# Layer 1's head outputs scaled and turned by VectorE, placed by DMA, with the gates written into the tiles of the gated outputs

## The chip, the cores and the metric

One core of a Trainium2 chip runs the whole program in one launch. The metric is the device time of that launch in microseconds (us). Before the change it was 1343.44 us, the median of 3 runs (1340.47 to 1344.24).

## The reference, cut to what matters

The program is one step of a trunk with two layers, on 512 prompt tokens and 32 sample tokens, 1024 wide, in float32. Layer 0 is an RWKV-7 layer and layer 1 is a differential attention layer with 12 heads of 128. Only layer 1 is touched:

```python
def diff_layer(x, mk, mv, k_past, v_past, layer_idx, norm_w, w_out, w_in, ...):
    h = rmsnorm(x, norm_w)
    q, k, v, qm, gate = jnp.split(h @ w_in, [...], axis=-1)
    ...
    attn = probs(q1, k1) - lam * probs(q2, k2)
    o = einsum('bhqk,bkhd->bqhd', attn, v_all)
    o = rmsnorm(o, subln) * (1.0 - lam_init)
    y_mem = mem_attention(qm, mk, mv)
    out = jnp.concatenate([o, y_mem], axis=-1) * jax.nn.silu(gate)
    return x + out @ w_out, k, v
```

What the change concerns is the last part: each head's output `o` (512 tokens by 128 values) is divided by its root mean square, turned from token-major to value-major, multiplied by `subln` and by the gate, and then used in the product with `w_out`. The four memory heads (`y_mem`) share the same engines and queues.

## The kernel before, in words

**Projections.** A projection of 128 columns is one `block` (L1947): its weights come in two loads of 256 KB each (`load`, L271; tile `raw`, five buffers), ScalarE rounds each half to a short form (`whi`), VectorE subtracts to get the rest (`wlo`; `split`, L300, two buffers of each, one buffer is a whole block's weights), and TensorE runs 48 matmuls `ps_g` of 272 columns: two halves of the tokens, eight slices of the depth, and three products for each (high by high, high by low, low by high). A `raw` buffer may be loaded again once the `wlo` made from it has been written.

**Pieces between matmuls.** The other work of layer 1 is cut into steps (Python generators), and `block` runs a step ahead of the matmul whose number is listed for it, so `step(end, 8)` means: the next step of `end` ahead of the block's matmul 8. TensorE and SyncE are "tied" in this layer (`tie`, L123): they keep the order in which the program was written. For VectorE and ScalarE the tile framework's scheduler picks the order. On the chip each engine then works through its list in order, and SyncE, which issues nearly all DMAs, does so too.

**Groups.** `groups` (L1958) runs three groups of four heads. In each, the key, query and value blocks of the four heads come first, and the attention of a head (scores `ps_s`, softmax, transposes `ps_aT`, product `ps_o`) is spread over the blocks that follow. Then come the blocks of gates. In groups 0 and 1: gate of head 0, query of a first memory head, gates of heads 1 and 2, query of a second memory head, gate of head 3, and the gates of the two memory heads. In group 2 there are no memory heads: gates of heads 0 to 3, after which the product with `w_out` begins, and the ties of TensorE and SyncE are lifted after the gate of head 0.

**The sample tokens.** `diff_end` (L2253) handles the 32 sample tokens of the four heads together: softmax of their scores `ssb`, transposes `ps_saT`, the product `ps_os`, its root mean square (a short chain of one-column steps on VectorE: `os`, `nt`), the scaling `os<-os,os`, a transpose `ps_osT` on TensorE, and a copy `osT`.

**The heads' outputs.** The last part of `diff_end`, here called fin, is asked once per head. VectorE scales the four 128x128 squares of the head's output `ot` by the reciprocal root mean squares (columns of `oss`), TensorE transposes the four squares into PSUM (`ps_oT`), and VectorE multiplies the result by `subs` (named `dv` in the profile's rows) and by the gate `sg` into the gated output `og` (the tile `o1[g]`, 128 values by 544 tokens); a small product does it for the sample tokens. The gate itself (`gate_evac`, L1072) is written by ScalarE (tanh) and VectorE into one of two buffers `sg`.

**Memory heads.** `mem_steps` (L1252) makes the scores of a memory head in three tiles (`ps_mm`: two tiles of 256 tokens, and one of the samples with `cmk`), their softmax (`mnm`, `mp`, `mrs`), and for the first two tiles a transposition in squares of 32 by VectorE (`mpq`). `placed` (L131) writes such a tile to DRAM with four DMAs that put every square of 32 where it belongs (scratch `mprob`), and one DMA fetches the whole turned tile (`mpT`). The product `ps_mo` takes `mpT` with the memory values `mhv` and `cmv`, whose loads SyncE issues beside them. `small_out` and `moved` in `diff_head` (L2056) turn attention probabilities in the same way.

Of the kernel before, what the change touches and what calls it, by code (L numbers as in the profile page):

```python
# [9 lines left out]
F32 = mybir.dt.float32  # L10
# [4 lines left out]
ALU = mybir.AluOpType  # L15
AX = mybir.AxisListType

P = 128
D = 1024
KT = D // P  # L20
TP = 512
# [4 lines left out]
MIXW = 1536  # L26
# [12 lines left out]
SGB = 2  # L39
# [69 lines left out]
class Trunk:  # L109
# [962 lines left out]
    def gate_evac(self, n):  # L1072
        nc = self.nc
        sg = self.sg[n % SGB]

        def evac(ps, v):
            self.ae.activation(sg[:, v], ps, AF.Tanh, scale=0.5)
            gated = lambda: self.ve.scalar_tensor_tensor(sg[:, v], sg[:, v], 1.0, ps, ALU.add, ALU.mult)
            if not self.ordered:
                return gated()  # L1080
            done.append(self.put_off(gated, 0.43))
            return gated

        done = []

        def get():
            self.until(done[-1])
            return sg

        return sg, get, evac  # L1090

    def gate(self, src, c0):

        self.gates += 1
        sg, _, evac = self.gate_evac(self.gates)
        self.proj(src, c0, evac)
        return sg

    def dest(self, g, sg):

# [390 lines left out]
    def layer0(self, mem):  # L1491
        nc, o = self.nc, self.o
        w = self.a["rw_in"][0]
# [4 lines left out]
        with ExitStack() as ctx:  # L1498
# [43 lines left out]

            def add_gate(pr, st, c0, n):
                def make(wt):
                    sg, st["gate"], evac = self.gate_evac(n)
                    yield from self.steps(wt, evac)
                add(pr, w, c0, make)

# [19 lines left out]
            mems, came, made = [{} for _ in range(MH)], [], {}  # L1568
# [104 lines left out]
            for pr in range(NPAIR):  # L1673
# [9 lines left out]
                t, left, spent = 0.0, each[pr] - kept, 0.0  # L1683
# [156 lines left out]
    def layer1(self):  # L1840
# [7 lines left out]
        with ExitStack() as ctx:  # L1848
            with ExitStack() as c2:
                self.dfp = p = self.pool("df", 1, ctx=c2)  # L1850
                m1 = c2.enter_context(ExitStack())
                mp = self.pool("mem1a", 1, ctx=m1, side="right")

                nlam = self.nlam
                self.vscr = [self.dp.tile([TP, P], F32, name=f"vscr{i}") for i in range(2)]
                self.ascr = [self.dp.tile([TP, P], F32, name=f"ascr{i}") for i in range(4)]
                self.bscr = [self.dp.tile([3 * P, P], F32, name=f"bscr{i}") for i in range(2)]
                self.mprob = [self.dp.tile([TP, P], F32, name=f"mprob{i}") for i in range(4)]
                self.qs = [p.tile([P, P], F32, name=f"qs{i}") for i in range(2)]
                for t in self.qs:  # L1860
                    nc.gpsimd.memset(t[:], 0.0)  # L1861
                self.kz = [p.tile([P, 2, T], F32R, name=f"kz{i}") for i in range(2)]
                for t in self.kz:
                    for m in range(2):
                        r = slice(64 - 64 * m, P - 64 * m)
                        nc.gpsimd.memset(t[r, m, :].bitcast(F32), 0.0)
                pe, early = [], iter(order[:MADE])

                def aside():
                    if pe:  # L1870
                        made.update({g: self.gated(g, *self.fetch(pe[0], g)) for g in islice(early, 2)})

                def free():
                    m1.close()
                    pe.append(self.pool("wo1e", 1, ctx=ctx, side="right"))

                self.groups(w, p, mp, nlam, aside, free)
# [65 lines left out]
            for _ in self.w_out(1, p, order, consume, o=made)[0]:  # L1943
                pass
        self.hctx.close()

    def block(self, w, c0, evac, pieces=()):  # L1947
# [10 lines left out]
    def groups(self, w, p, mp, nlam, aside, free):  # L1958

        late = []  # L1960
        for hg in range(3):
            gr = self.diff_group(hg, p)
            heads = [self.diff_head(gr, j, p, nlam) for j in range(4)]
            sgs, fins, prev = [], [], None
            step = lambda it, *at: [(i, lambda: next(it, None)) for i in at]

            turns = lambda it, last: step(last, 2) + step(it, 6) + step(last, 10) + step(it, 20, 26) + step(last, 30) + step(it, 36, 47)

            def gate(c0, pieces):
                self.gates += 1  # L1970
                sg, _, evac = self.gate_evac(self.gates)
                self.block(w, 3 * MIXW + 512 + c0, evac, pieces)
                return sg

            for j, (parts, it) in enumerate(heads):
                h = 4 * hg + j
                before = step(prev, 4, 14, 36, 42) if j else late
                if j > 1:
                    before = before[:2] + step(heads[j - 2][1], 22, 30) + before[2:]
                k, q, v = parts()  # L1980
                self.block(w, MIXW + h * P, k, before)
                if not j and hg == 2:
                    free()
# [12 lines left out]
                prev = it  # L1996
            end = self.diff_end(gr, nlam)
            fin = lambda j, at: (at, lambda: end.send((j, sgs[j])))
            g0 = 4 * hg * P
            sgs.append(gate(g0, step(prev, 4, 14) + step(heads[2][1], 22, 30) + step(prev, 36, 42)))  # L2000
# [20 lines left out]
            sgs.append(gate(g0 + P, step(prev, 4) + step(end, 8) + step(prev, 14) + step(end, 28)))  # L2021
            sgs.append(gate(g0 + 2 * P, step(m0, 14, 14) + step(end, 16) + [fin(0, 22)] + step(m0, 28, 28) + step(m1, 30, 30) + [fin(1, 38)]))
            self.block(w, 3 * MIXW + st1["c"], query(st1), step(m0, 4, 14, 14) + step(m1, 20) + step(m0, 28, 40))
            sgs.append(gate(g0 + 3 * P, [fin(2, 10)] + step(m1, 22, 22, 36, 36)))
            sg0 = gate(MIXW + st0["c"], [fin(3, 10)])
            st0["gate"] = lambda sg0=sg0: sg0
            sg1 = gate(MIXW + st1["c"], step(m0, 8) + step(m1, 16, 26, 26, 38))
            st1["gate"] = lambda sg1=sg1: sg1
            late = step(m1, 8, 22)

# [222 lines left out]
    def diff_end(self, gr, nlam):  # L2253
# [39 lines left out]
        ask = yield  # L2293
        while True:
            j, sg = ask
            on = gr["on"][j]
# [8 lines left out]
            ask = yield  # L2305

    def combine(self, pt, rs, n, nlam):

# [78 lines left out]
```

## Time and profile before

| | |
|---|---|
| median of 3 runs | 1343.44 us |
| the profiled execution's own time | 1343.22 us |
| its span | 1341.3 us |
| mean granted TensorE clock | 0.997 |
| instructions in the trace | 31455 |
| DMA packets, bytes | 472324, 170.78 MB |

The profile is of one execution. Its times count in us from the start of the span. Each row of a timeline has the start, the length, the engine (PE is TensorE, DVE is VectorE, ACT is ScalarE, SPq is SyncE's issuing of DMAs), the line, the operation with what it writes and reads, and how many instructions of the kind follow one another (x). Where the engine stood still ahead of a row, the idle time and what ended it stand in brackets. Nearly all rows have line 106, since a helper records the operations, so the tile names tell them apart. Matmuls are pipelined: a row's length overlaps the next row, and what a matmul costs is the distance between starts.

### The profile page before, as it was taken

The numbers are of one execution on the slowest core, as the hardware profiler recorded it, in microseconds if no ns is written. First come the engines' busy times: TensorE is split into PE (matmuls) and PEld (weight loads), VectorE is DVE, ScalarE is ACT, GpSimd is POOL, SyncE is SP. The second block draws the span as 40 slices with busy tenths as digits, with TensorE's granted clock in tenths as the row PEclk, the third lists the DMA queues.
The fourth block names the chain that finished last, engine by engine and source line by source line (L and its number), as shares of the span: only waits on it lengthen the run. The fifth ranks groups of instructions, "written<-read, shape, count | busy, mean of one in ns | idle before, by whom it ended". The sixth has DMA issues, their size and how long they took to land. (4 is left out here: it accounts for less than half of the span.)

```text
span 1341.3 us, 31455 instructions
## 1 busy us (share of the span) xinstructions
PE 1305.8 (97%) x11507; PEld 1248.3 (93%) x11507; DVE 975.8 (73%) x2393; ACT 797.3 (59%) x2244; POOL 364.0 (27%) x833
## 2 busy tenths in 40 slices
PE   8999999999999999999999999999999999999997
PEld 6988899999999998888999999999999999999997
DVE  5776788888888888675754478877588758887343
ACT  5765678877787777565543376654466536664222
POOL 2127668666776668600000000000000001002000
PEclk9999999999999999999999999999999999999999
DMA  7454344445443444443375466764487464872321
GB/s 226 146 146 108 90 105 99 103 104 119 95 118 91 115 113 99 113 141 90 99 197 135 128 199 154 164 154 119 113 185 178 100 159 111 184 158 89 95 84 71
DMA packets 472324, 170.78 MB, mean 127 GB/s; under 512 B 244857, under 2 KB 462722, under 8 KB 472170
## 3 DMA queue, kind: packets, MB, share of 16 engines
q1 hardware_dynamic: 472106, 168.76, 50.2%
q8 instruction: 91, 1.49, 0.5%
q14 instruction: 63, 0.52, 0.1%
q10 hardware_dynamic: 64, 0.02, 0.0%
HBM read 128.16 MB, written 40.34 MB: 126 GB/s over the span
## 5 line engine op out<-in xcount | busy, mean ns | idle before, releaser
L106 PE MATMUL ps_g<-hh,wlo 128*128 128x272 f32 x1808 | 537.0, 298 | 1.0 <-DVE wlo L106 0.9
L106 PE MATMUL ps_g<-hl,whi 128*128 128x272 f32 x1808 | 534.8, 297 | 1.0 <-DVE hl L106 0.7
L106 PE MATMUL ps_g<-hh,whi 128*128 128x272 f32 x1808 | 528.9, 293 | 1.2 <-DVE ats L106 0.8
L106 PEld LDWEIGHTS ps_g<-hh,whi 128*128 128x128 f32 x1808 | 341.0, 189 | 4.9 <-DVE ats L106 1.0
L106 PEld LDWEIGHTS ps_g<-hl,whi 128*128 128x128 f32 x1808 | 340.7, 189 | 5.0 <-DVE hl L106 1.9
L106 PEld LDWEIGHTS ps_g<-hh,wlo 128*128 128x128 f32 x1808 | 340.5, 189 | 3.1 <-DVE wlo L106 1.7
L106 DVE TENSOR_TENSOR wlo<-raw,whi 128x512 fp32r<-128x512 f32 x314 | 215.5, 698 | 102.2 <-ACT whi L106 99.9
L106 ACT CAST whi<-raw 128x512 fp32r<-128x512 f32 x314 | 189.0, 619 | 117.0 <-PE ps_g L106 56.0
L881 POOL TENSOR_TENSOR tm<-u,m 102x84 f32<-102x84 f32 (+23 forms) x341 | 143.4, 421 | 118.8 <-DMA m<-sc 67.8
L883 POOL TENSOR_TENSOR u<-u,tm 102x84 f32<-102x84 f32 (+23 forms) x341 | 152.8, 448 | 26.7
L106 PE MATMUL ps_g<-hi,wlo 128*128 128x272 f32 x512 | 147.7, 288 | 1.4 <-DVE wlo L106 1.4
L106 PE MATMUL ps_g<-hi,whi 128*128 128x272 f32 x512 | 147.8, 289 | 0.0
L106 PE MATMUL ps_g<-lo,whi 128*128 128x272 f32 x512 | 147.5, 288 | 0.0
L1390 POOL TENSOR_TENSOR lo<-og,hi 128x544 fp32r<-128x544 f32 x8 | 13.2, 1653 | 374.2 <-ACT hi L106 373.8
L106 PEld LDWEIGHTS ps_g<-hi,wlo 128*128 128x128 f32 x512 | 96.4, 188 | 1.8 <-DVE wlo L106 1.8
L106 PEld LDWEIGHTS ps_g<-hi,whi 128*128 128x128 f32 x512 | 96.5, 189 | 0.2 <-ACT whi L106 0.2
L106 PEld LDWEIGHTS ps_g<-lo,whi 128*128 128x128 f32 x512 | 96.4, 188 | 0.2 <-DVE lo L106 0.2
L106 ACT ACTIVATE pt<-ps_s,snm 128x128 f32<-128x128 f32 (+3 forms) x96 | 50.3, 527 | 63.7 <-DVE snm L106 63.7
L106 DVE SCALAR_TENSOR_TENSOR SB<-ps_c,dl,sd 64x64 f32<-64x64 f32 x168 | 47.4, 282 | 23.3 <-PE ps_c L106 21.0
L106 ACT COPY sv<-ps_c 64x64 f32<-64x64 f32 x192 | 39.6, 206 | 33.7 <-PE ps_c L106 31.8
L106 ACT ACTIVATE sg<-ps_g 128x272 f32<-128x272 f32 x64 | 25.1, 394 | 45.7 <-PE ps_g L106 41.4
L1861 POOL MEMSET qs<- 128x128 f32 x2 | 0.3, 205 | 190.6 <-PE ps_g L106 190.6
(399 smaller groups left out, 2480.5 us busy)
## 6 DMA issues: line engine op xcount, KB each, us to landing
raw<-in_rw_in_dram SPq DMA_DIRECT2D x114, 256.0 KB
raw<-in_df_in_dram SPq DMA_DIRECT2D x112, 256.0 KB
raw<-in_w_out_dram SPq DMA_DIRECT2D x64, 256.0 KB
tscr<-bt SPq DMA_DIRECT2D x48, 128.0 KB
bt<-tscr SPq DMA_DIRECT2D x12, 512.0 KB
oscr<-sg SPq DMA_DIRECT2D x16, 272.0 KB
lo<-oscr SPq DMA_DIRECT2D x16, 272.0 KB
m<-sc SPq DMA_DIRECT2D x33, 128.0 KB
```

The source lines that it names most:

```text
L106: return lambda *a, **k: self.trunk.tie(self, issue(*a, **k))
L881: nc.gpsimd.tensor_tensor(tm[:, :n, :wd], u3[:, :n, kx : kx + 1].to_broadcast(sh), m3[:, kx : kx + 1, kx + 1 :].to_broadcast(sh), ALU.mult)
L883: nc.gpsimd.tensor_tensor(u3[:, :n, kx + 1 :], u3[:, :n, kx + 1 :], tm[:, :n, :wd], ALU.add)
L1390: (self.nc.gpsimd if g % 2 and self.o1 else self.ve).tensor_tensor(lo[:], t, hi[:].bitcast(F32), ALU.subtract)
L1861: nc.gpsimd.memset(t[:], 0.0)
```

## The change

- The gate of a head is written straight into `o1[g]`, and the final products work in place there. The ring `sg` is no longer used in layer 1, for the memory heads either.
- fin is replaced by `diff_out`, which has four steps a head. *turn*: one VectorE product of 128x512 scales all four squares by a broadcast operand, and one VectorE transposition in squares of 32 writes `oq` (a buffer of the ring of three that `mpq` and `aT` use too). *put*: `placed` writes `oq` to DRAM (`oturn`) with four DMAs of 64 KB. *land*: one DMA of 256 KB fetches the turned tile back into `ot`. *fin*: VectorE multiplies `ot` by `subs` and the gate, and does the sample tokens' small product.
- With it 48 transposes `ps_oT` leave TensorE (and their 48 scalings of 128x128 leave VectorE), and 60 DMAs come to SyncE's queue: 12 heads by four puts and one landing.
- In group 2 the ties now hold until after the gate of head 3, `diff_end` starts at matmul 8 of the gate of head 1 in place of matmul 2 of the gate of head 2, and the fin steps of heads 2 and 3 run inside the `w_out` product (at its matmuls 6 and 24).

```diff
@@ groups
-            def gate(c0, pieces):
-                self.gates += 1
-                sg, _, evac = self.gate_evac(self.gates)
+            def gate(c0, pieces, g):
+                sg, _, evac = self.gate_evac(self.o1[g][:])
...
+            did = lambda what, j, at: [(at, lambda: self.diff_out(gr, what, j))]
+            own = lambda j, pieces: gate(g0 + j * P, pieces, 4 * hg + j)
+            own(0, step(prev, 4, 14) + step(heads[2][1], 22, 30) + step(prev, 36, 42))
             if hg == 2:
+                own(1, step(prev, 4) + step(end, 8) + step(prev, 28, 40, 46))
+                aside()
+                own(2, step(end, 2) + did("turn", 0, 18) + did("turn", 1, 26) + did("put", 0, 32) + did("turn", 2, 34) + step(end, 38) + did("put", 1, 40))
+                own(3, did("put", 2, 0) + did("turn", 3, 6) + did("land", 0, 8) + did("land", 1, 14) + did("put", 3, 18) + did("land", 2, 22)
+                    + did("fin", 0, 34) + did("land", 3, 40) + did("fin", 1, 44))
                 self.te.tied = self.se.tied = False
-                sgs.append(gate(g0 + P, step(prev, 4, 28, 40, 45)))
-                aside()
-                sgs.append(gate(g0 + 2 * P, step(end, 2, 10, 18) + [fin(0, 22), fin(1, 36)]))
-                sgs.append(gate(g0 + 3 * P, [fin(2, 16)]))
-                fin(3, 0)[1]()
+                self.last = did("fin", 2, 6) + did("fin", 3, 24)
                 break
...
@@ diff_end, diff_out
-            for t in range(4):
-                self.ve.tensor_scalar(on[:, t, :], on[:, t, :], ss[:, 2, 4 * j + t : 4 * j + t + 1], None, ALU.mult)
-            ps = self.psm.tile([P, 512], F32, tag="m", name="ps_oT")
-            for t in range(4):
-                self.te.transpose(ps[:, t * P : t * P + P], on[:, t, :], self.ident[:])
-            g = self.dest(4 * hg + j, sg)
-            self.ve.scalar_tensor_tensor(g[:, :TP], ps[:], self.subs, sg[:, :TP], ALU.mult, ALU.mult)
-            self.ve.tensor_tensor(g[:, TP:], oT[:, 32 * j : 32 * j + 32], sg[:, TP:], ALU.mult)
+        if what == "turn":
+            r = gr["ss"][:, 2, 4 * j : 4 * j + 4].unsqueeze(2).to_broadcast([P, 4, P])
+            self.ve.tensor_tensor(on[:], on[:], r, ALU.mult)
+            x = gr["x", j] = self.dfp.tile([P, 512], F32, tag="aT", name="oq", bufs=3)
+            self.ve.transpose(x[:], on[:].rearrange("p t d -> p (t d)"))
+        elif what == "put":
+            self.placed(scr[:], gr["x", j][:])
+        elif what == "land":
+            self.se.dma_start(on[:], scr[:].rearrange("(t p) q -> p t q", p=P))
+        else:
+            self.ve.scalar_tensor_tensor(g[:, :TP], on[:].rearrange("p t q -> p (t q)"), self.subs, g[:, :TP], ALU.mult, ALU.mult)
+            self.ve.tensor_tensor(g[:, TP:], gr["oT"][:, 32 * j : 32 * j + 32], g[:, TP:], ALU.mult)
```

The order of the instructions moves on other engines too. The first place is ScalarE in group 0, at the gates of the two memory heads (`sg`, or `og_12240` and `og_12241` now), around the softmax of the second memory head's last score tile (`mp,mrs<-ps_mm,mnm`). Before:

```order
L106 CAST whi<-raw 128x512 x2
L106 ACTIVATE sg_83<-ps_g 128x272
L106 CAST whi<-raw 128x512
L106 ACTIVATE sg_83<-ps_g 128x272
L106 CAST whi<-raw 128x512
L106 ACTIVATE sg_83<-ps_g 128x272
L106 ACTIVATE mp,mrs<-ps_mm,mnm 128x256
L106 CAST whi<-raw 128x512
L106 ACTIVATE sg_83<-ps_g 128x272
L106 CAST whi<-raw 128x512
L106 COPY mpS<-ps_mt_14430 128x64
```

And now:

```order
L106 CAST whi<-raw 128x512 x2
L106 ACTIVATE og_12240<-ps_g 128x272 x2
L106 ACTIVATE og_12241<-ps_g 128x272
L106 ACTIVATE mp,mrs<-ps_mm,mnm 128x256
L106 CAST whi<-raw 128x512 x2
L106 ACTIVATE og_12241<-ps_g 128x272
L106 COPY mpS<-ps_mt_14430 128x64
```

The pair of weight casts that stood ahead of that last softmax tile stands behind it now. On VectorE the `wlo` of these casts moves with them, and so does the time at which their `raw` buffers come free for SyncE's loads, whose place in SyncE's list, ahead of `mhv`, `cmv`, `mpT` and the last `mprob` and `mpT`, is as it was.

The second place is VectorE in group 0, where the sample outputs are scaled (`os<-os,os`) for `ps_osT`. Before:

```order
L106 SCALAR_TENSOR_TENSOR os_13875<-nt_13879,os_13875 128x1
L106 TENSOR_SCALAR ot<-ot,oss 128x128
L106 TENSOR_SCALAR os<-os,os_13875 128x128
L106 TENSOR_TENSOR wlo<-raw,whi 128x512
L106 SCALAR_TENSOR_TENSOR sg_83<-sg_83,ps_g 128x272
L106 TENSOR_TENSOR wlo<-raw,whi 128x512
L106 TENSOR_SCALAR ot<-ot,oss 128x128 x2
L106 TENSOR_REDUCE mnm<-ps_mm 128x2
```

And now:

```order
L106 SCALAR_TENSOR_TENSOR os_13879<-nt_13883,os_13879 128x1
L106 SCALAR_TENSOR_TENSOR og_12229<-og_12229,ps_g 128x272
L106 TENSOR_TENSOR nt_13883<-os_13879 128x1
L106 TENSOR_TENSOR wlo<-raw,whi 128x512
L106 TENSOR_TENSOR nt_13883<-nt_13883,os_13879 128x1
L106 TENSOR_TENSOR wlo<-raw,whi 128x512
L106 SCALAR_TENSOR_TENSOR nt_13883<-nt_13883 128x1
L106 TENSOR_REDUCE mnm<-ps_mm 128x2
L106 SCALAR_TENSOR_TENSOR os_13879<-nt_13883,os_13879 128x1
L106 TENSOR_SCALAR os<-os,os_13879 128x128
```

The scaling of `os` stood ahead of two `wlo`, a gate product and the reduction `mnm` of a memory head's first scores; now it stands behind them. In group 2 two scalings of 128x512, one `oq` transposition and one gate product have come between the chain and the scaling of `os`, where one scaling of 128x128 stood.

The third place is TensorE in group 2, in the gate of head 1, from the transposes of the last head's third tile of probabilities on. Before:

```order
L106 MATMUL ps_g<-hh,whi 128x272
L106 MATMUL ps_g<-hl,whi 128x272
L106 MATMUL ps_saT<-ident,ssb 128x128
L106 MATMUL ps_saT<-ident,ssb 32x128
L106 MATMUL ps_g<-hh,wlo 128x272
```

And now:

```order
L106 MATMUL ps_aT<-ident,pt 128x128 x3
L106 MATMUL ps_g<-hl,whi 128x272
L106 MATMUL ps_g<-hh,wlo 128x272
L106 MATMUL ps_g<-hh,whi 128x272
L106 MATMUL ps_g<-hl,whi 128x272
L106 MATMUL ps_saT<-ident,ssb 128x128
L106 MATMUL ps_saT<-ident,ssb 32x128
L106 MATMUL ps_g<-hh,wlo 128x272
```

The transposes of the samples' probabilities followed the same `ps_aT x3` after 46 `ps_g` and four more `ps_aT`; now they follow it after 4 `ps_g`. The transpose `ps_osT` further on stands 36 `ps_g` behind `ps_os`, where it stood 31 behind.

More of the change, by code (lines that the diff above doesn't have):

```diff
@@ L1070, in state_out, with gate_evac @@
         self.se.dma_start(dst.rearrange("h v k -> (h v) k"), so[:])
-    def gate_evac(self, n):
-        nc = self.nc
-        sg = self.sg[n % SGB]
+    def gate_evac(self, sg):
         def evac(ps, v):
@@ L1090, in gate_evac @@
         return sg, get, evac
-    def gate(self, src, c0):
-        self.gates += 1
-        sg, _, evac = self.gate_evac(self.gates)
-        self.proj(src, c0, evac)
-        return sg
     def dest(self, g, sg):
@@ L1544, in make @@
                 def make(wt):
-                    sg, st["gate"], evac = self.gate_evac(n)
+                    sg, st["gate"], evac = self.gate_evac(self.sg[n % SGB])
                     yield from self.steps(wt, evac)
@@ L1856, in layer1 @@
                 self.ascr = [self.dp.tile([TP, P], F32, name=f"ascr{i}") for i in range(4)]
+                self.oturn = [self.dp.tile([TP, P], F32, name=f"oturn{i}") for i in range(4)]
                 self.bscr = [self.dp.tile([3 * P, P], F32, name=f"bscr{i}") for i in range(2)]
@@ L1941, in finish @@
                     self.se.dma_start(o[0][0, i * P : i * P + P, :] if i < 4 else o[1][0], ys[i][n, :])
-            for _ in self.w_out(1, p, order, consume, o=made)[0]:
-                pass
+            for i, _ in enumerate(self.w_out(1, p, order, consume, o=made)[0]):
+                while self.last and self.last[0][0] <= i:
+                    self.last.pop(0)[1]()
         self.hctx.close()
@@ L1963, in groups @@
             heads = [self.diff_head(gr, j, p, nlam) for j in range(4)]
-            sgs, fins, prev = [], [], None
+            prev = None
             step = lambda it, *at: [(i, lambda: next(it, None)) for i in at]
             turns = lambda it, last: step(last, 2) + step(it, 6) + step(last, 10) + step(it, 20, 26) + step(last, 30) + step(it, 36, 47)
-            def gate(c0, pieces):
-                self.gates += 1
-                sg, _, evac = self.gate_evac(self.gates)
+            def gate(c0, pieces, g):
+                sg, _, evac = self.gate_evac(self.o1[g][:])
                 self.block(w, 3 * MIXW + 512 + c0, evac, pieces)
@@ L1997, in groups @@
             end = self.diff_end(gr, nlam)
-            fin = lambda j, at: (at, lambda: end.send((j, sgs[j])))
+            did = lambda what, j, at: [(at, lambda: self.diff_out(gr, what, j))]
             g0 = 4 * hg * P
-            sgs.append(gate(g0, step(prev, 4, 14) + step(heads[2][1], 22, 30) + step(prev, 36, 42)))
+            own = lambda j, pieces: gate(g0 + j * P, pieces, 4 * hg + j)
+            own(0, step(prev, 4, 14) + step(heads[2][1], 22, 30) + step(prev, 36, 42))
             if hg == 2:
-                self.te.tied = self.se.tied = False
-                sgs.append(gate(g0 + P, step(prev, 4, 28, 40, 45)))
-                aside()
-                sgs.append(gate(g0 + 2 * P, step(end, 2, 10, 18) + [fin(0, 22), fin(1, 36)]))
-                sgs.append(gate(g0 + 3 * P, [fin(2, 16)]))
-                fin(3, 0)[1]()
+                own(1, step(prev, 4) + step(end, 8) + step(prev, 28, 40, 46))
[3 more added lines that the diff above has]
+                    + did("fin", 0, 34) + did("land", 3, 40) + did("fin", 1, 44))
+                self.te.tied = self.se.tied = False
+                self.last = did("fin", 2, 6) + did("fin", 3, 24)
                 break
@@ L2020, in groups @@
             self.block(w, 3 * MIXW + st0["c"], query(st0), step(m0, 2) + step(prev, 4, 40))
[L2021 to L2025, printed above, removed]
+            own(1, step(prev, 4) + step(end, 8) + step(prev, 14) + step(end, 28))
+            own(2, step(m0, 14, 14) + step(end, 16) + did("turn", 0, 20) + step(m0, 28, 28) + step(m1, 30, 30) + did("put", 0, 36) + did("turn", 1, 38))
+            self.block(w, 3 * MIXW + st1["c"], query(st1), step(m0, 4) + did("put", 1, 6) + step(m0, 14) + did("land", 0, 14) + step(m0, 14)
+                       + did("turn", 2, 16) + step(m1, 20) + step(m0, 28) + did("land", 1, 32) + did("put", 2, 34) + did("turn", 3, 36) + step(m0, 40)
+                       + did("fin", 0, 42))
+            own(3, did("put", 3, 4) + did("land", 2, 10) + did("fin", 1, 12) + step(m1, 22, 22) + did("land", 3, 30) + step(m1, 36, 36) + did("fin", 2, 38))
+            sg0 = gate(MIXW + st0["c"], did("fin", 3, 12), 12 + 2 * hg)
             st0["gate"] = lambda sg0=sg0: sg0
-            sg1 = gate(MIXW + st1["c"], step(m0, 8) + step(m1, 16, 26, 26, 38))
+            sg1 = gate(MIXW + st1["c"], step(m0, 8) + step(m1, 16, 26, 26, 38), 13 + 2 * hg)
             st1["gate"] = lambda sg1=sg1: sg1
@@ L2292, in diff_end, with diff_out @@
         self.ae.activation(oT[:], psT[:, :P], AF.Copy, scale=self.subs)
[L2293 to L2296, printed above, removed]
-            for t in range(4):
-                self.ve.tensor_scalar(on[:, t, :], on[:, t, :], ss[:, 2, 4 * j + t : 4 * j + t + 1], None, ALU.mult)
-            ps = self.psm.tile([P, 512], F32, tag="m", name="ps_oT")
-            for t in range(4):
-                self.te.transpose(ps[:, t * P : t * P + P], on[:, t, :], self.ident[:])
-            g = self.dest(4 * hg + j, sg)
-            self.ve.scalar_tensor_tensor(g[:, :TP], ps[:], self.subs, sg[:, :TP], ALU.mult, ALU.mult)
-            self.ve.tensor_tensor(g[:, TP:], oT[:, 32 * j : 32 * j + 32], sg[:, TP:], ALU.mult)
-            ask = yield
+        gr["oT"] = oT
+        yield
+    def diff_out(self, gr, what, j):
+        on, scr, g = gr["on"][j], self.oturn[j], self.o1[4 * gr["hg"] + j]
+        if what == "turn":
[10 more added lines that the diff above has]
+            self.ve.tensor_tensor(g[:, TP:], gr["oT"][:, 32 * j : 32 * j + 32], g[:, TP:], ALU.mult)
     def combine(self, pt, rs, n, nlam):
```

## Prediction

> **What bounds the kernel now.** I read the page's busy times first:
>
> ```profile
> PE 1305.8 (97%) x11507; PEld 1248.3 (93%) x11507; DVE 975.8 (73%) x2393; ACT 797.3 (59%) x2244; POOL 364.0 (27%) x833
> ```
>
> TensorE works 97% of the 1341.3 us span. The table by stretches, asked for layer 1, sharpens it (columns: stretch, length; busy time and instructions of TensorE, its weight loads, VectorE, ScalarE, GpSimd; granted clock, DMA share, GB/s):
>
> ```profile
> 850.00:900.00 50.00, 50.00 (x400) 49.63 (x398) 39.21 (x108) 31.52 (x100) 0.00 (x0) 1.00 0.70 163
> 900.00:950.00 50.00, 50.00 (x381) 47.24 (x381) 32.16 (x93) 19.14 (x61) 0.00 (x0) 1.00 0.52 131
> ```
>
> TensorE has no idle time there, VectorE 18 of 50 us in the stretch in which group 0's outputs are finished. So two things count and nothing else: what TensorE no longer has to do, at full price, and every moment at which TensorE, in its fixed order, comes to an instruction whose input isn't there. The rest was to find such moments: I went along TensorE's new order and asked of each input when the trace of before has it ready.
>
> **The change, part by part.** *TensorE's work.* A head's four transposes, in TensorE's timeline:
>
> ```profile
> 910.30 0.29 PE L106 MATMUL ps_g<-hh,whi 128*128 128x272 f32 x1
> 910.44 0.60 PE L106 MATMUL ps_oT<-ident,ot 128*128 128x128 f32 x4
> 910.79 0.37 PE L106 MATMUL ps_g<-hl,whi 128*128 128x272 f32 x1
> 911.00 0.29 PE L106 MATMUL ps_g<-hh,wlo 128*128 128x272 f32 x1
> 911.12 0.29 PE L106 MATMUL ps_g<-hh,whi 128*128 128x272 f32 x1
> ```
>
> Plain matmuls start 0.125 us apart (911.00 to 911.12). From 910.30 to 911.00 pass 0.70 us for two of them and the four transposes, so these cost 0.70 - 0.25 = 0.45 us a head, and 12 heads 5.4 us. In group 2 the transposes also wait for VectorE:
>
> ```profile
> 1222.32 0.30 PE L106 MATMUL ps_osT<-ident,os 128*128 128x128 f32 x1
> ...
> 1223.59 0.37 PE L106 MATMUL ps_g<-hh,wlo 128*128 128x272 f32 x1
> 1224.36 0.88 PE L106 MATMUL ps_oT<-ident,ot 128*128 128x128 f32 x3 [0.40 <-DVE ot L106]
> 1225.20 0.39 PE L106 MATMUL ps_g<-hh,whi 128*128 128x272 f32 x1
> ```
>
> 1223.59 to 1225.20 is 1.61 us, where a matmul and three quarters of 0.45 make 0.46: some 1.2 us go as well. Gain: -6.6 us.
>
> *VectorE's work* hardly changes:
>
> ```profile
> L106 DVE TENSOR_SCALAR ot<-ot,oss x48: 263/277/283, 905.1 to 1228.6; 128x128 f32<-128x128 f32 x48
> L106 DVE STREAM_TRANSPOSE mpq<-mp x8: 697/704/714, 913.0 to 1088.9; 128x512 f32<-128x512 f32 x8
> ```
>
> (shortest, median, longest in ns). A head had 4 x 0.28 of scaling; it gets one product like `mp<-mp,mrs` (0.68 in the row at 912.07, below) and one transposition of 0.70. That is 0.3 us more a head beside 18 idle in 50, so the load is priced at nothing; what matters is in which order it stands, next.
>
> *Wait A: `ps_osT` in groups 0 and 1.* The scaling of `os` has moved behind the reduction `mnm`. Timelines of VectorE and TensorE:
>
> ```profile
> 907.43 0.28 DVE L106 TENSOR_SCALAR os<-os,os 128x128 f32<-128x128 f32 x1
> 909.57 0.68 DVE L106 TENSOR_REDUCE mnm<-ps_mm 128x2 f32<-128x512 f32 x1
> 912.07 0.68 DVE L106 TENSOR_TENSOR mp<-mp,mrs 128x512 f32<-128x512 f32 x1
> 912.67 0.42 DVE L106 SCALAR_TENSOR_TENSOR sg<-sg,ps_g 128x272 f32<-128x272 f32 x1
> ```
>
> ```profile
> 909.57 0.27 PE L106 MATMUL ps_osT<-ident,os 128*128 128x128 f32 x1
> ```
>
> TensorE asks for `os` at 909.57 and had it 1.9 us early. `mnm` can't start much sooner than 909.57, since four scalings of 0.60 (912.07 to 912.67, the distance between starts) now fill the time in which four of 0.28 stood, and so `os` is done some 0.60 + 0.1 + 0.28 = 1.0 later, at 910.55; with the wake-up TensorE stands 1.1. Twice: +2.2 (bounds 0.5 to 2.6).
>
> *Wait B: the second memory head's `ps_mo`, groups 0 and 1.* The pair of weight casts has moved behind the last softmax tile. ScalarE, VectorE and SyncE of before:
>
> ```profile
> 937.07 0.62 ACT L106 CAST whi<-raw 128x512 fp32r<-128x512 f32 x1 [2.52 <-PE ps_g L106]
> 943.63 0.47 ACT L106 ACTIVATE mp<-ps_mm,mnm 128x256 f32<-128x256 f32 x1 [0.90 <-DVE mnm L106]
> ```
>
> ```profile
> 944.43 0.43 DVE L106 TENSOR_TENSOR mp<-mp,mrs 128x256 f32<-128x256 f32 x1
> ```
>
> ```profile
> 932.10 6.71 SPq L106 DMA_DIRECT2D raw<-in_df_in_dram  x4
> 939.87 0.34 SPq L106 DMA_DIRECT2D mhv<-mkv  x1
> 940.31 0.39 SPq L106 DMA_DIRECT2D cmv<-in_cache_mem_v_dram  x1
> 940.79 0.42 SPq L106 DMA_DIRECT2D mpT<-mprob  x1
> 941.26 2.21 SPq L106 DMA_DIRECT2D mprob<-mpq  x4
> 945.39 0.38 SPq L106 DMA_DIRECT2D mpT<-mprob  x1
> ```
>
> ```profile
> 948.57 1.02 PE L106 MATMUL ps_mo<-mpT,mhv 128*128 128x512 f32 x2
> ```
>
> The first cast of the pair ran at 937.07, its `wlo` behind it, and the fourth `raw` load, which takes the buffer that this `wlo` frees, was issued by 938.8. Now the cast comes after the softmax at 943.63, which waits for TensorE's scores: it ends at about 944.8, and its `wlo`, behind `mp` (944.86) and itself some 0.6 like the products of 128x512 above, at 945.5. SyncE stands at that load until then, with `mhv`, `cmv`, `mpT` and `mprob` queued behind it. From there by the rows: load 0.45, `mhv` 0.44, `cmv` 0.48, `mpT` 0.47, so the last `mprob` starts at 947.3, and 941.26 to 945.39 says that the last `mpT` leaves 4.13 later, at 951.5. Its flight: in group 0 of before it was under 3.2 (945.39 to 948.57, no wait); group 1 shows one that TensorE waited for:
>
> ```profile
> 1101.45 0.38 SPq L106 DMA_DIRECT2D mpT<-mprob  x1
> ```
>
> ```profile
> 1104.40 0.29 PE L106 MATMUL ps_g<-hh,whi 128*128 128x272 f32 x1
> 1105.12 0.70 PE L106 MATMUL ps_mo<-mpT,mhv 128*128 128x512 f32 x1 [0.43 <-DMA mpT<-mprob]
> ```
>
> That is 3.7. I take 3.0 in group 0: the data are there at 954.5, wanted at 948.57, so TensorE stands 5.9 us. In group 1 the old wait (1104.40 + 0.125 to 1105.12, 0.6) is part of it: +5.3. Together +11.2. From below: were the load not held at all, nothing would be left; with half the hold, 3 each. From above, with 3.7 of flight, 6.6 and 6.0. I take the value near the rows, since every step of the chain stands in one queue. SyncE's added puts and landings are hidden in this sum by the same hold.
>
> *Wait C: group 2.* TensorE comes to `ps_saT` 4 matmuls after `ps_aT`, where before 46 and other work lay between:
>
> ```profile
> 1203.83 0.49 PE L106 MATMUL ps_aT<-ident,pt 128*128 128x128 f32 x3
> ...
> 1204.53 0.29 PE L106 MATMUL ps_g<-hl,whi 128*128 128x272 f32 x1
> ...
> 1210.36 0.38 PE L106 MATMUL ps_saT<-ident,ssb 128*128 128x128 f32 x2
> ```
>
> ```profile
> 1207.36 0.43 DVE L106 SCALAR_TENSOR_TENSOR sg<-sg,ps_g 128x272 f32<-128x272 f32 x1
> 1207.71 0.16 DVE L106 RECIPROCAL srs<-srs 128x2 f32<-128x2 f32 x1
> ...
> 1208.44 0.39 DVE L106 SCALAR_TENSOR_TENSOR ssb<-ssb,srs 128x160 f32<-128x160 f32 x1
> ```
>
> It asks at 1204.65. `ssb` was ready at 1208.83, and the gate product at 1207.36 no longer stands ahead of it (0.35): 1208.48. TensorE stands 3.8 us (bounds 2.5 to 4.2). Further on, `ps_osT` comes 5 matmuls, 0.6 us, later than before, and `os` about 0.60 + 0.60 + 0.70 + 0.35 - 0.28 = 2.0 later, for two scalings, an `oq` transposition and a gate product ahead of it in place of one small scaling: +1.4 (bounds 0 to 2). The turned tiles of heads 2 and 3 are first used inside the `w_out` product, with tens of matmuls in between; I cost that at nothing, and 0.5 if that cover is gone.
>
> Sum: -6.6 + 2.2 + 11.2 + 3.8 + 1.4 = +12.0 us. On the profiled execution's 1343.2 that is 1355.2; the median is 0.2 above it, so I give 1355.4.
>
> **The clock.** The tail of before shows what long standstills of TensorE do:
>
> ```profile
> 1333.60:1337.00 3.40, 0.00 (x0) 0.00 (x0) 3.13 (x10) 2.05 (x3) 0.00 (x0) 1.00 0.36 137
> 1337.00:1341.00 4.00, 0.00 (x0) 0.00 (x0) 0.06 (x1) 0.00 (x0) 0.00 (x0) 0.50 0.69 245
> ```
>
> After 3.4 us without a matmul the granted clock is half. [...]
>
> **Rivals.** *The clock halves.* Waits of 5.9 and 5.3 (B) can hold such a stretch, 3.8 (C) hardly. [...] For it: the rows above. [...] Chance 0.25, and it is on the same side.
>
> *B is not there.* If SyncE's load isn't held (the wait falls on an older `wlo`), only A and C are left: -6.6 + 2.2 + 5.2 = +0.8, 1344.2. Against it: in before the fourth load was issued right behind that `wlo`'s turn. Chance 0.08.
>
> *Faster.* VectorE, no longer halted by `ps_oT` and the ring `sg`, runs ahead of its old times at all four places, and the inputs are there when TensorE comes. If all waits go, -6.6 is left: 1336.8. It decides where the waits together stay under 2.6 us, since 4.0 us is the bound below. For it: VectorE has 18 idle in 50. Against it: A, B and C hang on scores that TensorE itself makes shortly before, so being ahead doesn't help. Chance 0.09.
>
> **How the numbers follow.** A measurement of this kernel can tell 0.3%, 4.0 us, from no change. My forecast, 1355.4, has 0.58 (its own range by the bounds: 1347.5 to 1358), the clock 0.25, no B 0.08, faster 0.09. The range leaves out faster and nearly all of "no B": 1346.5 to 1361. Slower by over 4 us is nearly all of forecast and clock: 0.82; within 4 us "no B" and the low edge of the forecast: 0.09; faster: 0.09.
>
> **What would show it.** Right: no `ps_oT` rows; TensorE's idle time in front of `ps_mo` of the second memory head, some 5 to 6 us twice, ended by the DMA of `mpT`; 1 us twice in front of `ps_osT` and 3.8 us once in front of `ps_saT`, ended by VectorE; SyncE's last `mpT` of a group some 6 us later against TensorE. Wrong: `ps_mo` without a wait, or the casts and the fourth load at their old times; then the sum falls by 5 us a place, and a fall in time proves the rival without waits. Half a granted clock behind the waits would prove the clock.

## The result, and the profile after

The changed kernel took 1367.59 us (median of 5 runs, 1364.13 to 1369.02) beside 1343.44 for the kernel before: 1.0172 times as long, with a 95% interval of 1.0153 to 1.0192. That is 24 us slower, where 12 were forecast: the side was right, and the forecast was half of the size. The profiled execution took 1367.59 us, with a span of 1365.5 and a mean granted clock of 0.987.

TensorE's table of waits after the change has the forecast places at its head (columns: what waited, on what; us in total, times, longest):

```profile
PE ps_mo L106 <- DMA mpT<-mprob: 14.8, 2, 7.8
...
PE ps_saT L106 <- DVE ssb L106: 3.8, 1, 3.8
PE ps_osT L106 <- DVE os L106: 3.6, 3, 1.5
...
PE ps_g L106 <- DVE lo L106: 1.4, 1, 1.4
```

The first three are B, C and A of the prediction. The last one, in the output product, was priced at nothing there, and at 0.5 without cover. TensorE's timeline at the first of them, in group 0:

```profile
948.74 0.28 PE L106 MATMUL ps_g<-hh,whi 128*128 128x272 f32 x1
956.78 3.78 PE L106 MATMUL ps_mo<-mpT,mhv 128*128 128x512 f32 x4 [7.76 <-DMA mpT<-mprob]
960.36 0.90 PE L106 MATMUL ps_mo<-mpS,cmv 128*128 128x32 f32 x4
...
961.44 0.43 PE L106 MATMUL ps_g<-hh,wlo 128*128 128x272 f32 x1
961.67 0.43 PE L106 MATMUL ps_g<-hh,whi 128*128 128x272 f32 x1
```

The reader sees a wait of 7.8 us, and then that the plain matmuls start 0.23 us apart in place of 0.125. The table by stretches of the same kernel (columns as in the prediction; the third from the right is the granted clock) says why:

```profile
949.00:952.00 3.00, 0.03 (x1) 0.00 (x0) 0.48 (x1) 0.00 (x0) 0.00 (x0) 1.00 0.99 238
952.00:956.70 4.70, 0.00 (x0) 0.00 (x0) 0.00 (x0) 0.00 (x0) 0.00 (x0) 0.50 0.45 108
...
957.70:961.00 3.30, 3.30 (x8) 1.66 (x6) 0.40 (x1) 0.00 (x0) 0.00 (x0) 0.50 0.60 191
961.00:965.00 4.00, 4.00 (x29) 4.00 (x29) 0.47 (x2) 0.39 (x1) 0.00 (x0) 0.84 0.00 0
...
1121.00:1125.00 4.00, 3.29 (x4) 1.51 (x5) 0.00 (x0) 0.00 (x0) 0.00 (x0) 0.50 0.87 258
...
1226.30:1230.00 3.70, 3.56 (x16) 3.53 (x17) 0.00 (x0) 0.00 (x0) 0.00 (x0) 0.50 0.61 153
```

The clock is halved during the wait and stays so for some 5 us after TensorE resumes: of the stretch from 961 to 965 the mean of 0.84 leaves 1.3 us at half, so until about 962.3. The same is seen in group 1 (1121) and behind `ps_saT` in group 2 (1226), whose wait was only 3.8 us. SyncE's queue ahead of the first wait:

```profile
935.97 1.94 SPq L106 DMA_DIRECT2D oturn<-oq  x4
...
940.83 2.96 SPq L106 DMA_DIRECT2D mprob<-mpq  x4
943.83 2.33 SPq L106 DMA_DIRECT2D raw<-in_df_in_dram  x4
...
948.03 3.46 SPq L106 DMA_DIRECT2D mprob<-mpq  x4
953.91 0.38 SPq L106 DMA_DIRECT2D mpT<-mprob  x1
```

The four weight loads end at 946.2 and the last `mprob` starts at 948.03; forecast were 945.5 for the fourth load and 947.3 for that `mprob`. The times fit, but the reason is another than the one forecast. SyncE comes to the four loads only at 943.83, behind the puts, the landings and the first `mprob`, and is through with them in 2.33 us; in before it came to them at 932.10. Here the held load adds little to a queue that is late already. From the start of the last `mprob` to the last `mpT` pass 5.88 us (948.03 to 953.91), where before 4.13 did. The DMA share in the 5 us from there was 0.91, against 0.68 in before's:

```profile
948.00:953.00 5.00, 1.03 (x9) 0.81 (x7) 1.48 (x3) 0.64 (x2) 0.00 (x0) 0.90 0.91 212
```

```profile
941.20:946.20 5.00, 5.00 (x40) 4.95 (x39) 1.36 (x4) 1.47 (x4) 0.00 (x0) 1.00 0.68 146
```

At the output product, VectorE's timeline has the reason for the 1.4 us:

```profile
1256.15 3.97 DVE L106 SCALAR_TENSOR_TENSOR og<-ot,dv,og 128x512 f32<-128x512 f32 x3 [1.79 <-DMA ot<-oturn]
1261.42 0.75 DVE L106 SCALAR_TENSOR_TENSOR og<-ot,dv,og 128x512 f32<-128x512 f32 x1 [1.29 <-DMA ot<-oturn]
1262.09 3.21 DVE L106 TENSOR_TENSOR lo<-og,hi 128x544 fp32r<-128x544 f32 x4
```

The final products of group 2 wait for the landings on VectorE, and the splits `lo` that TensorE needs first are queued behind them.

### The profile page after: what moved, and what is told of

It reads as the page before. It is cut to its first block, busy times and chain, and to the rows that moved or that the text cites. A ratio compares the mean times of both kernels' runs of the same rounds, so it can differ in the third digit from the quotient of the medians.

```text
span 1365.5 us, 31413 instructions
## 1 busy us (share of the span) xinstructions
PE 1307.4 (96%) x11459; PEld 1249.0 (91%) x11459; DVE 979.6 (72%) x2369; ACT 797.4 (58%) x2244; POOL 363.8 (27%) x833
## 5 line engine op out<-in xcount | busy, mean ns | idle before, releaser
L106 DVE TENSOR_REDUCE snm<-ps_s 128x1 f32<-128x128 f32 (+3 forms) x96 | 42.9, 472 | 0.9
```

The lines of the kernel that those rows point to most:

```text
L106: return lambda *a, **k: self.trunk.tie(self, issue(*a, **k))
```

## The experiments

Two questions were open. What makes `mpT` late: the casts that hold SyncE's load (the prediction's mechanism), or SyncE's queue, which the added DMAs fill? And is the other half of the loss the clock? The theory: waits at fixed places of TensorE's list, made by late entries in SyncE's queue, and a halved clock behind each long one. The rivals stand in the expectations. Each ratio is to runs of the kernel before on the same chip; a time set against the changed kernel's is a difference of medians, and can be off by 1 to 2 us, since the chips differ (medians of before from 1342.84 to 1344.4).

**Without placing.**

```diff
-            self.placed(scr[:], gr["x", j][:])
+            pass
...
-            self.se.dma_start(on[:], scr[:].rearrange("(t p) q -> p t q", p=P))
+            pass
```

> The changed kernel without the 60 placing and landing DMAs (the final product reads the scaled but unturned tile, so the heads' outputs are left unturned). VectorE's work and TensorE's list stay. In this kernel the scheduler also puts the weight casts of group 0 and 1 back ahead of the last softmax tile. Theory (waits plus clock): both waits of about 7 us ahead of ps_mo go, with the 2 us of half clock behind each, and the wait of 1.4 us in the output product goes: 1367.6 - 14.9 - 4 - 1.4 = about 1347; the waits at ps_osT (1.0, 1.0, 1.5) and ps_saT (3.8) stay. Rival (the waits have nothing to do with SyncE's DMAs but with VectorE's and ScalarE's order alone): no placing changes little, over 1360.

Measured: 1348.24 us, 1.0027 (1.0013 to 1.0042). In the table of waits those at `ps_mo` have fallen to 0.8 in total; those at `ps_saT` (3.8) and `ps_osT` (4.6, where 3.6 were) stay:

```profile
PE ps_mo L106 <- DMA mpT<-mprob: 0.8, 1, 0.8
```

So the 60 DMAs, by load or by place, carry some 19 us of the 24. Which of the two this kernel can't tell, nor whether the casts count, since the scheduler has put them back.

**Without placing, casts late.** The split of the block's weights is called behind the last softmax tile, and each cast is ordered behind it.

```diff
-            todo.append((lambda k=k, q=q: self.ae.copy(hi[:, k], raw[q][:]), 0.0))
+            todo.append((lambda k=k, q=q: self.behind(self.ae.copy(hi[:, k], raw[q][:])), 0.0))
...
+    def behind(self, ins):
+        if getattr(self, 'exp', None):
+            self.order(ins, self.exp)
+        return ins
...
```

> The kernel without the 60 DMAs again (heads' outputs left unturned), but with the two weight casts ordered behind the last softmax tile of the second memory head, as the changed kernel has them. It tells the prediction's mechanism apart (the casts hold SyncE's fourth load, and what is queued behind it) from the rival that SyncE's queue is late only because of the added DMAs. Prediction's mechanism: ps_mo waits for mpT by 5 to 6 us in groups 0 and 1, 1347 + 11 + up to 3 for the clock = 1358 to 1361. Rival: as without placing, 1347, with no wait at ps_mo.

Measured: 1367.04 us, 1.0165 (1.0143 to 1.0186). SyncE's queue, and the wait:

```profile
933.05 1.97 SPq L106 DMA_DIRECT2D mprob<-mpq  x4
935.06 13.37 SPq L106 DMA_DIRECT2D raw<-in_df_in_dram  x4
...
950.01 2.59 SPq L106 DMA_DIRECT2D mprob<-mpq  x4
955.02 0.38 SPq L106 DMA_DIRECT2D mpT<-mprob  x1
```

```profile
957.71 1.22 PE L106 MATMUL ps_mo<-mpT,mhv 128*128 128x512 f32 x1 [6.42 <-DMA mpT<-mprob]
```

The four loads take 13.4 us, some 11 of it standing: in the next kernel four that nothing holds take 2.09. The prediction's mechanism alone is enough for 6.4 and 7.0 us of wait, with not one added DMA in the program. The total is above the expectation: the waits came to 13.5 where 11 were allowed, and the kernel without placing was itself 1 us above its expectation; the rest is put down to the clock (0.55 from 955 to 960 in the profiled execution, 0.77 from 960 to 965), which was not tried in this kernel.

**Loads behind the chain.** In groups 0 and 1 the loads of one block are issued at matmul 39 of the last memory gate, behind the last `mpT`.

```diff
-            sg1 = gate(MIXW + st1["c"], step(m0, 8) + step(m1, 16, 26, 26, 38), 13 + 2 * hg)
+            sg1 = gate(MIXW + st1["c"], step(m0, 8) + step(m1, 16, 26, 26, 38) + [(39, lambda: self.used(3))], 13 + 2 * hg)
...
```

> The changed kernel whole, but two of the four weight loads that stand in SyncE's queue ahead of mhv, cmv, mpT and the last mprob are issued behind the last mpT, in groups 0 and 1. So the late casts no longer hold the chain; the added DMAs ahead of it stay. Prediction's mechanism alone (the hold): the waits at ps_mo nearly vanish, about 1350. The two causes side by side (the queue is itself late because of eight more puts and two landings, up to 943.8): the waits shrink from 7.8 and 7.0 by the hold's 1 to 3 us each only, 1361 to 1365. Queue alone: no change, 1367.

Measured: 1360.4 us, 1.0121 (1.01 to 1.0143), waits at `ps_mo` of 5.7 and 4.4:

```profile
936.58 1.96 SPq L106 DMA_DIRECT2D oturn<-oq  x4
938.64 1.89 SPq L106 DMA_DIRECT2D ot<-oturn  x2
940.62 3.74 SPq L106 DMA_DIRECT2D mprob<-mpq  x4
944.40 1.18 SPq L106 DMA_DIRECT2D raw<-in_df_in_dram  x2
945.68 0.45 SPq L106 DMA_DIRECT2D mhv<-mkv  x1
...
947.23 2.75 SPq L106 DMA_DIRECT2D mprob<-mpq  x4
952.37 0.38 SPq L106 DMA_DIRECT2D mpT<-mprob  x1
952.85 2.09 SPq L106 DMA_DIRECT2D raw<-in_df_in_dram  x4
```

With no held load, the put of head 3 (936.58, 2.5 us behind the end of the load ahead of it) and the landing behind it make the queue nearly as late: the last `mprob` starts at 947.23, where 948.03 was the time in the changed kernel. The two causes stand side by side; each alone holds `mpT` for 4 us and more. The last row is four loads that nothing holds: they take 2.09 us, and the changed kernel's took 2.33. So in its group 0 the hold itself was some 0.2 us, hidden behind the added DMAs, and not the other way round. In its group 1 the four took 3.92, a hold of some 1.8.

**Waits filled.** Useless matmuls on TensorE ahead of the three long waits.

```diff
-            late = step(m1, 8, 22)
+            late = step(m1, 8) + [(22, lambda: self.fill(48))] + step(m1, 22)
...
-                own(1, step(prev, 4) + step(end, 8) + step(prev, 28, 40, 46))
+                own(1, step(prev, 4) + [(8, lambda: self.fill(24))] + step(end, 8) + step(prev, 28, 40, 46))
...
```

> The changed kernel with useless matmuls (into a PSUM buffer that nobody reads) on TensorE ahead of the three long waits: 48 of 272 columns ahead of ps_mo in groups 0 and 1 (6 us), 24 ahead of ps_saT in group 2 (3 us). They take no time from anyone if TensorE stands there anyway. If the granted clock halves because of the standstill, it stays at 1.00 and the half-speed time behind each wait goes: 2.1 + 2.1 + 1.7 = 6 us, 1361.5. If the clock has nothing to do with it, 1367.6 or more.

Measured: 1361.37 us, 1.0122 (1.0101 to 1.0143), and a mean clock of 0.996 in place of 0.987. By stretches and in TensorE's timeline:

```profile
952.00:957.00 5.00, 4.17 (x32) 3.72 (x31) 0.00 (x0) 0.00 (x0) 0.00 (x0) 1.00 0.51 136
957.00:961.00 4.00, 3.92 (x24) 2.98 (x23) 0.78 (x2) 0.39 (x1) 0.00 (x0) 1.00 0.60 183
```

```profile
949.55 6.08 PE L106 MATMUL ps_fill<-hh 128*128 128x272 f32 x48
956.46 1.98 PE L106 MATMUL ps_mo<-mpT,mhv 128*128 128x512 f32 x4 [0.83 <-DMA mpT<-mprob]
```

`ps_mo` begins as late as before the filling, but its four products take 1.98 us in place of 3.78. 120 matmuls more, and the kernel is 6.2 us faster by the medians; beside its own runs of before it loses 17.0, where the changed kernel loses 24.2. The clock's share of the loss is 6 to 7 us.

**The samples' transposes later.** `diff_end` yields once more behind the softmax, and `ps_saT` comes at matmul 36.

```diff
-                own(1, step(prev, 4) + step(end, 8) + step(prev, 28, 40, 46))
+                own(1, step(prev, 4) + step(end, 8) + step(prev, 28) + step(end, 36) + step(prev, 40, 46))
...
```

> The changed kernel with the transposes ps_saT of group 2 put at matmul 36 of the gate of head 1 in place of matmul 8; the softmax of ssb stays at 8. TensorE then reaches ps_saT some 4.5 us after ps_aT x3, ssb needs 3.8. Theory: the wait of 3.8 us goes, and with it the half clock of some 1.7 us behind it: 1367.6 - 5.5 = about 1362. Rival without the clock: 1363.7. Rival (the wait only moves to ps_os or ps_osT, since VectorE's chain sets the end): 1366 or more.

Measured: 1357.65 us, 1.0116 (1.0099 to 1.0133). The wait at `ps_saT` is gone and nothing took its place. The profiled execution, at 1360.8 the slowest of its four, is 6.8 us shorter than the changed kernel's. Of this, 1.3 lie ahead of layer 1's first `ps_aT`, which starts at 880.7 in place of 882.0 and is not touched by the edit; from there to the end it is 5.4 us, as expected (5.5). Layer 0 varies by itself: from 129.5 to 136.2 us the changed kernel's profiled execution had a granted clock of 0.50 and this one 1.00. That the median fell by 9.9 isn't explained beyond that.

**Puts spread.** The put of head 2 behind the memory head's first `mprob`, the put of head 3 among the weight loads, the landings behind the last `mpT`, the final products behind them; in group 2 the last two final products come at matmuls 40 and 60 of the output product.

```diff
-            own(3, did("put", 3, 4) + did("land", 2, 10) + did("fin", 1, 12) + step(m1, 22, 22) + did("land", 3, 30) + step(m1, 36, 36) + did("fin", 2, 38))
-            sg0 = gate(MIXW + st0["c"], did("fin", 3, 12), 12 + 2 * hg)
+            own(3, did("fin", 1, 12) + step(m1, 22, 22) + did("turn", 2, 30) + step(m1, 36, 36) + did("put", 2, 38))
+            sg0 = gate(MIXW + st0["c"], did("turn", 3, 10) + did("put", 3, 20), 12 + 2 * hg)
...
```

> The changed kernel whole, with the turns, puts, landings and final products of heads 2 and 3 in groups 0 and 1 moved behind what the second memory head needs: put of head 2 behind the first mprob of that head, put of head 3 among weight loads that wait anyway, both landings behind the last mpT, final products in the next group's first block. The scheduler then puts the casts ahead of the last softmax tile again. All 60 DMAs stay. Theory (place in the queues, not the amount of traffic): both waits at ps_mo shrink to under 1 us, and the half clock goes, 1367.6 - 19 = about 1348.5, as without placing. Rival (traffic): the waits stay at 3 us or more, 1355 or more.

Measured: 1373.35 us, 1.0232 (1.0214 to 1.025), slower than the changed kernel, with waits of 10.0 and 9.5 at `ps_mo`. SyncE's queue:

```profile
935.79 1.14 SPq L106 DMA_DIRECT2D raw<-in_df_in_dram  x2
943.56 1.96 SPq L106 DMA_DIRECT2D oturn<-oq  x4
945.61 1.02 SPq L106 DMA_DIRECT2D raw<-in_df_in_dram  x2
```

SyncE stands from 936.9 to 943.56 at the put of head 3, whose turned tile VectorE's order brings late (its `oq` ends at 943.53), and the loads and the memory head's DMAs are behind it. The expectation failed, though not the idea that a late entry holds what is behind it: the casts were early again, and the held entry was another.

**All moved.** The same, with `ps_saT` and `ps_osT` later and group 2's puts ahead of its landings.

> The same, with ps_saT at matmul 36, ps_osT at matmul 34 of the gate of head 2 in groups 0 and 1 and at matmul 6 of the gate of head 3 in group 2, and group 2's puts ahead of all its landings. All waits that came in should be gone: theory 1343.4 - 6.6 = 1337 to 1340, faster than before. Rival (VectorE's and SyncE's extra work comes back as other waits): 1343 or more.

Measured: 1367.61 us, 1.0185 (1.0169 to 1.0201). The waits at `ps_saT` and `ps_osT` are gone; those at `ps_mo` are 9.6 and 10.0, as in the kernel ahead, and the one for `lo` grew to 3.3. It missed for the same reason.

**Puts behind.** Turns, puts and landings of heads 2 and 3 behind the last `mpT`.

```diff
+            bound = lambda what, j, at, gr=gr: [(at, lambda: self.diff_out(gr, what, j))]
+            late = bound("put", 2, 4) + step(m1, 8) + bound("turn", 3, 12) + bound("put", 3, 18) + step(m1, 22)
+            late = late + bound("land", 2, 30) + bound("land", 3, 40)
+            last = bound("fin", 2, 10) + bound("fin", 3, 20)
...
```

> The changed kernel whole, all 60 DMAs kept, but in groups 0 and 1 the turns, puts and landings of heads 2 and 3 come behind the last mpT in SyncE's queue (the turns at the end of the last memory gate and in the next group's first block, the final products in its second). In the spread version one put still stood ahead of the weight loads, mhv and the last mprob, and its turned tile came late from VectorE (it was issued at 943.6), so SyncE stood there in place of at the load. Theory (one late entry in SyncE's queue holds all behind it; the amount of traffic does not count): now the waits at ps_mo shrink to about 1 us each and the half clock behind them goes, 1367.6 - 14.9 - 4.4 + 1.5 = about 1350. Rival (60 DMAs more are too much for SyncE or the DMA engines at any place): waits of 3 us or more at ps_mo or at the next group's aT and weights, 1357 or more.

Measured: 1355.4 us, 1.0088 (1.0071 to 1.0105), between the two expectations.

```profile
PE ps_mo L106 <- DMA mpT<-mprob: 3.9, 2, 2.0
...
PE ps_saT L106 <- DVE ssb L106: 3.8, 1, 3.8
PE ps_osT L106 <- DVE os L106: 3.6, 3, 1.5
```

The same 60 DMAs, at another place in one queue, take 12 us off the changed kernel, so place and not the amount of traffic is most of it. But two things changed at once: in this kernel the scheduler put the pair of casts ahead of the last softmax tile again, so the hold is gone as well.

```profile
938.34 1.14 ACT L106 CAST whi<-raw 128x512 fp32r<-128x512 f32 x2
...
944.50 0.47 ACT L106 ACTIVATE mp<-ps_mm,mnm 128x256 f32<-128x256 f32 x1 [0.90 <-DVE mnm L106]
```

How the 12 us divide between the puts' place and the casts isn't shown. What is left at `ps_mo`, 2 us each, was not taken apart; in group 0 the last placing takes 5.14 us here (943.37 to 948.51), 1.0 more than in before.

**Two groups.** Groups 0 and 1 so, with `ps_osT` later; group 2 with TensorE's transposes as before.

> The same for groups 0 and 1, with ps_osT at matmul 34 of the gate of head 2 (behind VectorE's late scaling of os), and group 2 done as before: TensorE's transposes, ties lifted after the gate of head 0, gates in the tiles of the gated outputs. It keeps 8 heads of the saving, 8 x 0.45 = 3.6 us, and should have none of the waits: 1343.4 - 3.6 = 1339.8, if no other wait takes its place. Rival: other waits of 1 us and more come back in groups 0 and 1, 1342 to 1347.

Measured: 1348.61 us, 1.0036 (1.0022 to 1.0049). Waits of 2.5 and 2.2 remain at `ps_mo`, with half a clock in group 1 (0.51 from 1108.9 to 1112.3), and smaller ones came at `ps_s` (1.0 in total) and `ps_ck`: together more than the 3.6 saved. No version here that turns the heads' outputs by DMA beats the kernel before.

**The gates alone.**

```diff
-            def gate(c0, pieces):
-                self.gates += 1
-                sg, _, evac = self.gate_evac(self.gates)
+            def gate(c0, pieces, g):
+                sg, _, evac = self.gate_evac(self.o1[g][:])
```

> The kernel before with one part of the change: the gates are written into the tiles of the gated outputs (no ring of two buffers in layer 1), TensorE's transposes and all positions as before. Theory (the waits come from the placing and the positions): no change, 1343 within 2 us. Rival (writing the gates in place moves VectorE's order and makes part of the loss): 1347 or more.

Measured: 1343.31 us, 0.9997 (0.9984 to 1.0011). This part costs nothing that these runs can tell (2 us).

**Group 2 alone.**

```diff
-            own(2, step(m0, 14, 14) + step(end, 16) + did("turn", 0, 20) + step(m0, 28, 28) + step(m1, 30, 30) + did("put", 0, 36) + did("turn", 1, 38))
+            own(2, step(m0, 14, 14) + step(end, 16) + did("pe", 0, 22) + step(m0, 28, 28) + step(m1, 30, 30) + did("pe", 1, 38))
```

> One part of the change alone: group 2 as the changed kernel has it, groups 0 and 1 with TensorE's transposes at the positions of before (gates in the tiles of the gated outputs throughout). Theory: it loses what the changed kernel's group 2 loses by itself, the waits at ps_saT (3.8), at ps_osT (1.5) and ahead of the output product (1.2) and some 1.7 of half clock, and saves 4 x 0.45 + 1.2 = 3.0 us: 1343.6 + 8.2 - 3.0 = about 1349; the other 18 us of the changed kernel's loss then belong to groups 0 and 1. Rival (the parts are not additive, the waits in group 2 come only from delays handed on by groups 0 and 1): 1341 to 1344.

Measured: 1350.43 us, 1.0057 (1.0042 to 1.0071): group 2 loses 7.6 us by itself, more than the 5.2 of the expectation, and nothing handed on from groups 0 and 1 is needed for it. If the parts add up, what is left of the 24, 16 to 17, belongs to those groups; they were not tried alone.

**Without the transposes.** The kernel before, without `ps_oT`.

```diff
-            ps = self.psm.tile([P, 512], F32, tag="m", name="ps_oT")
-            for t in range(4):
-                self.te.transpose(ps[:, t * P : t * P + P], on[:, t, :], self.ident[:])
...
-            self.ve.scalar_tensor_tensor(g[:, :TP], ps[:], self.subs, sg[:, :TP], ALU.mult, ALU.mult)
+            self.ve.scalar_tensor_tensor(g[:, :TP], on[:].rearrange("p t d -> p (t d)"), self.subs, sg[:, :TP], ALU.mult, ALU.mult)
```

> The kernel before, without its 48 transposes ps_oT (the final product reads the scaled, unturned tile; the heads' outputs are left unturned); gates, positions and SyncE's queue as before. It prices the part of TensorE's work that the change removes: the prediction's 5.4 + 1.2 us gives 1336.8; if the waits of other engines are hidden behind the transposes, 1340 or more.

Measured: 1340.51 us, 0.9981 (0.9971 to 0.9992), a gain of 1 to 4 us. The profiled execution, the fastest of the kernel's runs, is 5.5 us shorter. New waits eat part of the 6.6:

```profile
PE ps_g L106 <- DVE sg L106: 1.6, 1, 1.6
```

## Why the prediction was right in its places and wrong in its size

By its own steps, with the changed kernel's rows:

- *TensorE's work*, -6.6: the work is gone, but what it is worth is less, 1 to 4 us where it was tried by itself. Mis-sized, and that too makes the forecast too low.
- *Wait A*, +2.2: 1.03 us each by the table of waits; 2.4 for the two where the distance between TensorE's starts is taken. Right, and by the place named; from the end of `os` to TensorE's start, the wake-up of the prediction, pass 0.14 us (911.41 to 911.55):

```profile
910.33 0.69 DVE L106 TENSOR_REDUCE mnm<-ps_mm 128x2 f32<-128x512 f32 x1
910.93 0.15 DVE L106 SCALAR_TENSOR_TENSOR os<-nt,os 128x1 f32<-128x1 f32 x1
911.12 0.29 DVE L106 TENSOR_SCALAR os<-os,os 128x128 f32<-128x128 f32 x1
```

- *Wait B*, +11.2: 14.8 - 0.4 = 14.4. The place is right; the step "SyncE stands at that load until then" is half of the cause. It is shown to be enough by itself (casts late alone: 6.4 and 7.0), but in the changed kernel SyncE stood there for some 0.2 us in group 0, since the puts and landings ahead had made it late already. The prediction took these to be hidden by the hold; it was the hold that was hidden by them, and without it they still cost 5.7 and 4.4. That both make SyncE late by nearly the same time, so that the forecast 947.3 came out as 948.03, is luck. The term that was mis-sized is the last placing: 4.13 us from its issue to the fetch in before, 5.88 now. Its DMA share is 0.91 instead of 0.68, with the four loads in one burst right ahead of it. The burst can't be all of the reason: in the kernels with late casts and with puts behind, where the loads are spread, the placing takes 5.01 and 5.14. Why it takes that long stays open.
- *Wait C*, +3.8 + 1.4: 3.8 and 1.5. Right.
- *The `w_out` product*, 0 (0.5 without cover): 1.4. The step "tens of matmuls in between" looked at the use of the late tiles themselves. TensorE waited for other tiles, which VectorE makes behind the final products in its list, and those stand waiting for the landings. Not all of the 1.4 is due to them: in the kernel without placing TensorE stood 1.0 us in the same product, for `wlo`.
- *The clock*: this is the step that failed. The sum has nothing for it; it was made a rival with 0.25, with "3.8 hardly". It came at all three places and cost 6 to 7 us together (the filled kernel), half of the 12 that are missing; a chance of 0.25 was too small. That a stretch without matmuls halves the clock was read rightly from the tail: in and behind the waits of 7.8, 7.0 and 3.8 us the granted clock was 0.50, and 1.00 around the first of them once it was filled with matmuls. The range's upper edge, 1361, has at most 1.7 us at each of three places for the clock (1355.4 + 5.1 = 1360.5), a term that no run shows. What the runs showed is some 2 us a place: TensorE resumed at 956.78 and was at half speed until about 962.3, over 5 us.

Summed with the measured terms and the whole 6.6: 2.4 + 14.4 + 5.3 + 1.4 + 6 - 6.6 = 22.9, of 24.2 by the two spans. With 1 to 4 for the transposes the same sum gives 25.5 to 28.5, so it closes only to within some 4 us. The forecast's own lower bound was added up wrongly: its lowest terms (0.5, 6.0, 2.5 and 0) give 1345.8 and not 1347.5; the outcome lies above the range, so nothing hangs on it.

## What to carry to other kernels

A change that takes work from the bound engine and gives it to a queue can be paid at the places where that queue is read in order (with the casts late, `mhv`, `cmv` and `mpT` stood behind 13.4 us of loads): look, for each late entry, at everything behind it. A wait of TensorE of 3.8 us and more cost its length and about 2 us again at half speed in the changed kernel, three times of three (6 to 7 us in all, by the filled kernel), so that price belongs in the sum and not among the rivals. And when two entries of a queue are late, removing one shows little: here each alone was enough for 4 us and more, and a forecast by one of them came near the right time for the wrong reason.

## What the runs showed of the hardware that was not expected

- 120 useless matmuls in the waits made the kernel 6 us faster (1361.37 against 1367.59): `ps_mo` begins as late as without them (956.46 and 956.78), and the granted clock is 1.00 behind the wait in place of 0.50.
- A wait of 1.95 us was followed by half a clock, where the tail of before was granted 1.00 through 3.4 us without a matmul. In the kernel with the puts behind, TensorE's timeline and the table by stretches show 1.95 us of waiting, and half speed after it:

```profile
951.53 2.95 PE L106 MATMUL ps_mo<-mpT,mhv 128*128 128x512 f32 x4 [1.95 <-DMA mpT<-mprob]
```

```profile
949.20:952.60 3.40, 1.45 (x7) 0.68 (x6) 0.00 (x0) 0.00 (x0) 0.00 (x0) 0.97 0.83 243
952.60:955.00 2.40, 2.40 (x8) 1.37 (x6) 0.48 (x1) 0.00 (x0) 0.00 (x0) 0.50 1.01 208
```

  A stretch of 3.4 us in which TensorE was busy for 1.45 was followed by half a clock; in group 1 of the same kernel it was 1.41 (1109.40 to 1112.80), with 0.51 behind it. A wait of 2.5 us in group 0 of the kernel with two groups was not followed by half a clock (1.00 from 947.0 to 953.0), so the length of the wait alone doesn't decide it; what else does was not shown.
